# Encoder trunk on one core: the second half's root factors written as rows, and the pace of the last hidden pair

## Chip, cores and metric

One core of one Trainium2 chip. The metric is the time of one execution on the device in microseconds (us), as the median of several executions; three were made of the kernel before.

## What is computed

One layer of a streaming encoder for 2048 prompt frames and 32 sample frames of 1024 channels, everything in float32. The reference, cut to what matters here:

```python
def rmsnorm(x, g):
    y = x * lax.rsqrt(jnp.mean(x * x, axis=-1, keepdims=True) + EPS)
    return y * g

def layer(x, ...):
    h = rmsnorm(x, g_pre_mix)
    z = h @ w_in                      # u | zq | zf | zi | zg
    y_pool = pool_mix(u_ext, ...)     # trailing means over 2/4/8/16 frames, a 128x128 map per group
    S1, o = hgrn_run(S0, q, kin, zi, logf)   # gated recurrence in chunks, 4 heads of 128
    y_hg = rmsnorm(o, g_hg_norm) * silu(zg)
    x = x + rmsnorm(concat([y_pool, y_hg]) @ w_out, g_post_mix)
    h2 = rmsnorm(x, g_pre_ffn)
    f = (silu(h2 @ w_gate) * (h2 @ w_up)) @ w_down
    return x + rmsnorm(f, g_post_ffn)
```

The number that this case turns on is the root of the first `rmsnorm`: one factor `1/sqrt(mean(x*x) + EPS)` for each frame.

## The kernel before

The frames go through in two halves of 1024 frames (the second with the 32 sample frames beside it). For each half: the normed input in channel layout, split into a high and a low float32r part (`hT`); the value columns of `w_in` (`first_values` for the first half, `values` for the second); for each of 4 heads the gate, query and output-gate columns and the recurrence (`head_products`, `hgrn`); the pooling groups (`pool_products`); the projection by `w_out` in two groups of four tiles and two column halves (`project`, L1025); and gate and up of the feed-forward by a seven-product scheme (`gate_up`, L1201). When both halves are done, `down` (L1496) multiplies by `w_down`. A float32 product is made of three float32r matmuls of 128x512 each.

**Order of the work.** TensorE's instructions stand in the order in which the Python code emits them. `mm` (L199) and `tick` (L196) add a planned duration to a counter, `Pace.t`, and every third matmul calls `poll` (L224), which lets each side task (a generator in a `Task`, L206) go one step when the time that it yielded has passed on that counter. The other engines' instructions and the DMA issues of SP are not bound to that order: the tile framework's scheduler puts them in the order in which it expects them to be ready, with their place in the code as priority. So a `yield` fixes where a step's TensorE instructions stand, and only moves the rest. Buffers come from pools: four PSUM banks from `mmbank`, four from `axbank` (L101), 21 slots of 128x512 from `t2` (L107).

**The roots.** For the first half they are made on the fly. For the second half a side task, `later_stats` (L465), runs during the first half: it loads the frames, sums their squares on ScalarE, and computes on GpSimd a tile `st[:, 24:32]` of 128x8, in which element (p, i) is the root of frame 128 i + p. It is written to a DRAM row `roots` (L489), and the 32 roots of the sample frames behind it (L490). In `front_norm` (L516) of the second half the row is loaded back, broadcast to all partitions (`rb`, L521), and VectorE multiplies the channels by it (`scaled_channels`, L506). Before L489 the task waits 100 us of the counter for nothing but its turn.

**The hidden factors.** When a pair of blocks of gate and up is done, `hidden` (L1156) makes from its four tiles the seven left factors of the down product: sums on VectorE (L1164 to L1174), a high part on ScalarE (`hhi`, L1178), a low part on VectorE (`hlo`, L1181), and a store of each to DRAM by SP (L1183, tiles `hdFalse` and `hdTrue` for the two halves). `gate_up` takes one such step in each slot; what is left at its end, 19 steps in either half, goes to a side task, `flush` (L1414), one step every 1400 ns of the counter. For the first half that task runs beside `values` of the second half, for the second half beside the start of `down`, whose left factors SP loads as `hst` (L1506).

In `values` (L648) the four PSUM banks of the first 512 frames must be copied out (L670, `va` and `vb`, two by ScalarE and two by VectorE) before the same four banks take the next 512 frames.

Of the kernel before, what the change touches and what calls it, by code (L numbers as in the profile page):

```python
# [16 lines left out]
P = 128  # L17
# [6 lines left out]
HALF = 1024  # L24
# [13 lines left out]
NCH = HALF // CHUNK  # L38
# [40 lines left out]
def body(tc, ins, outs, cst):  # L79
    nc = tc.nc  # L80
    ctx = ExitStack()
    with ctx:
# [18 lines left out]
        def axbank(name="axb"):  # L101
            return AX.tile([P, 512], F32, tag="ax", name=name)
# [4 lines left out]
        def t2(name, shape=None, dt=F32):  # L107
            return TP.tile(shape or [P, 512], dt, tag="t", name=name)
# [4 lines left out]
        ident = cons[:, C_ID:C_ID + P]  # L113
# [39 lines left out]
        roots = DP.tile([1, TMAX], F32, name="roots")  # L153
# [42 lines left out]
        def tick(ns):  # L196
            Pace.t += ns
# [120 lines left out]
        def sumsq(src, r, st):  # L318
            junk = SP.tile([P, D], BF16, tag="junk", name="junk", bufs=1)
            nc.scalar.activation(junk[0:r, 0:src.shape[1]], src, AF.Square, accum_out=st)  # L320
# [144 lines left out]
        def later_stats(S):  # L465

            st = S.st
            for i in range(NCH):
                for c in range(2):
                    x = t2("xtl")  # L470
                    r0 = S.tok0 + i * P
                    nc.sync.dma_start(out=x, in_=x_p[r0:r0 + P, c * 512:c * 512 + 512])
                    sumsq(x, P, st[:, 2 * i + c:2 * i + c + 1])
                    del x
                yield 20000.0
            xs = t2("xsl", [NS, 512]), t2("xsl", [NS, 512])
            for c in range(2):
                nc.sync.dma_start(out=xs[c], in_=x_s[:, c * 512:c * 512 + 512])
                sumsq(xs[c], NS, st[0:NS, 32 + c:33 + c])
            del xs  # L480
            yield 100000.0
            ev = st[:, 0:16].rearrange("p (i c) -> p i c", c=2)
            nc.gpsimd.tensor_tensor(st[:, 16:24], ev[:, :, 0], ev[:, :, 1], ALU.add)
            nc.gpsimd.tensor_scalar(st[:, 16:24], st[:, 16:24], 1.0 / D, EPS, ALU.mult, ALU.add)
            nc.gpsimd.tensor_tensor(st[:, 24:32], st[:, 16:24], nhalf[:, 0:1].broadcast_to([P, NCH]), ALU.pow)
            nc.gpsimd.tensor_tensor(st[0:NS, 34:35], st[0:NS, 32:33], st[0:NS, 33:34], ALU.add)
            nc.gpsimd.tensor_scalar(st[0:NS, 34:35], st[0:NS, 34:35], 1.0 / D, EPS, ALU.mult, ALU.add)
            nc.gpsimd.tensor_tensor(st[0:NS, 35:36], st[0:NS, 34:35], nhalf[0:NS, 0:1], ALU.pow)
            nc.sync.dma_start(out=roots[0, 0:HALF].rearrange("(i p) -> p i", p=P), in_=st[:, 24:32])  # L489
            nc.sync.dma_start(out=roots[0, HALF:TMAX].rearrange("(p i) -> p i", i=1), in_=st[0:NS, 35:36])  # L490

        def scaled_channels(S, tg):
# [708 lines left out]
        def gate_up(S, on_last):  # L1201
# [175 lines left out]
            def job():  # L1377
                if jobs and next(jobs[0], 0) == 0:
                    jobs.pop(0)
# [34 lines left out]
            def flush():  # L1414
                while jobs:
                    job()
                    yield 1400.0

            Task(flush())

        def residual(row0, r):
# [266 lines left out]
        with tc.manual_schedule(engines={mybir.EngineType.PE}):  # L1688
            for i, S in enumerate(halves):
                if i:  # L1690
                    while S.seen[0] < 1:
                        S.norm[0].step()
                    values(S, 0)
                    values(S, 1)
                if i == 0:
                    halves[1].st = CP.tile([P, 64], F32, name="st_b")
                    Task(later_stats(halves[1]), 25000.0)
                    Task(mixed_weights(), 4000.0)
                for h in range(NH):
                    head_products(S, h)  # L1700
                for g in (3, 2, 1, 0):
                    pool_products(S, g)
                S.gpm = row_vector("g_post_mix")
                for tg in range(2):
                    project(S, tg)
                gate_up(S, second_start if i == 0 else (lambda: down_first(halves)))
            down(halves)
            for tk in list(Pace.tasks):
                tk.finish()
# [40 lines left out]
```

## Time and profile before

| what | us |
|---|---|
| median of 3 executions | 2109.58 |
| lowest, highest | 2109.41, 2110.47 |
| the profiled execution's own time | 2110.55 |
| its span, first to last instruction | 2108.8 |

| engine | busy us | share of the span |
|---|---|---|
| TensorE matmul (PE) | 2081.5 | 99% |
| TensorE weight load (PEld) | 1690.4 | 80% |
| VectorE (DVE) | 1423.5 | 68% |
| ScalarE (ACT) | 831.6 | 39% |
| GpSimd (POOL) | 283.4 | 13% |

The profile is of one execution. "Idle before" in brackets is the time that an engine stood still before an instruction, with what ended that wait; "issue" means that nothing which the profile records ended it. PEclk is the clock that TensorE was granted, as a share of full speed: 1.00 is 2.4 GHz and 0.50 is 1.2 GHz. The DMA share is the mean busy share of the core's 16 DMA engines. SP's own rows are the issues of DMAs and not the transfers.

### The profile page before, as it was taken

The page shows a single profiled execution, that of the slowest core. Times are in us where ns is not written, and L with a number is a line of the kernel's source. Part 1 is how long each engine was busy: PE and PEld are TensorE (multiplying, and loading weights), DVE is VectorE, ACT ScalarE, POOL GpSimd, SP SyncE. Part 2 cuts the span into 40 slices and gives each one's busy share as a digit, 9 for nine tenths or more (in the row PEclk, how much of TensorE's full clock was granted, in tenths as well). Part 3 has the DMA queues.
Part 4 walks back from the last instruction along what each step waited for, and adds up shares of the span by engine and source line. Part 5 has one row for each costly group of instructions (what it writes and reads, how often), then busy time and mean ns, then how long its engine had stood idle before and what let it go on. Part 6 is the DMA issues. An engine that isn't in the chain of part 4 may idle for free.

```text
span 2108.8 us, 34100 instructions
## 1 busy us (share of the span) xinstructions
PE 2081.5 (99%) x13117; PEld 1690.4 (80%) x13117; DVE 1423.5 (68%) x2302; ACT 831.6 (39%) x1659; POOL 283.4 (13%) x387
## 2 busy tenths in 40 slices
PE   9999899999999999999999999999999999999998
PEld 8788688888888887778878788888888778888876
DVE  6565575797777778456575687767666856566587
ACT  6444344654444445233333664444444521011032
POOL 1132302200000000022231210000000301110134
PEclk9999999999999999999999999999999999999999
DMA  9321142626555557310014524545455796776778
GB/s 322 111 72 51 34 150 96 194 86 176 162 155 155 150 175 229 112 45 25 23 36 162 188 93 130 156 141 148 147 148 151 241 311 207 225 225 196 223 224 215
DMA packets 394242, 321.07 MB, mean 152 GB/s; under 512 B 19144, under 2 KB 321472, under 8 KB 394080
## 3 DMA queue, kind: packets, MB, share of 16 engines
q1 hardware_dynamic: 391632, 310.98, 47.9%
q0 software_dynamic: 2016, 7.34, 1.9%
q8 instruction: 104, 1.70, 0.3%
q10 hardware_dynamic: 432, 0.57, 0.1%
q14 instruction: 58, 0.48, 0.1%
HBM read 218.36 MB, written 100.47 MB: 151 GB/s over the span
## 4 chain that ended last, share of the span: by engine, by line
PE 88%; DVE 6%; issue 2%; DMA 1%; ACT 1%; POOL 1%; SPq 0%; DVEq 0%; POOLq 0%; ACTq 0%
PE gx L200 21%; PE mmb L200 15%; PE gy L200 10%; PE dx L200 10%; PE ops L200 10%; PE gz L200 5%; PE dy L200 5%; PE vps L200 3%; PE dz L200 2%; PE gb L200 1%; DVE acc L1533 1%; PE gw L200 1%; PE gsps L200 1%; PE ups L200 1%; PE tps L343 1%
## 5 line engine op out<-in xcount | busy, mean ns | idle before, releaser
L200 PE MATMUL gx<-fhi,wf 128*128 128x512 f32 x1376 | 387.3, 391 | 0.0
L200 PEld LDWEIGHTS gx<-fhi,wf 128*128 128x128 f32 x1376 | 256.6, 188 | 55.3 <-issue 3.0
L200 PE MATMUL gx<-flo,wf 128*128 128x512 f32 x688 | 213.0, 390 | 0.0
L200 PE MATMUL gy<-fhi,wf 128*128 128x512 f32 x704 | 201.8, 390 | 0.1
L200 PE MATMUL dx<-dhi,hst 128*128 128x512 f32 x640 | 185.3, 391 | 0.8 <-DVE acc L1533 0.6
L200 PE MATMUL mmb<-hTlo,whi 128*128 128x512 f32 x512 | 177.4, 407 | 0.0
L200 PE MATMUL mmb<-hThi,whi 128*128 128x512 f32 x512 | 166.4, 406 | 5.6 <-issue 5.6
L1533 DVE TENSOR_TENSOR acc<-dx,acc 128x512 f32<-128x512 f32 x168 | 115.0, 689 | 72.9 <-PE dx L200 72.1
L1256 DVE TENSOR_TENSOR wf<-s,wf 128x512 fp32r<-128x512 f32 x176 | 119.9, 687 | 60.6 <-ACT wf L1251 58.3
L200 PE MATMUL mmb<-hThi,wlo 128*128 128x512 f32 x512 | 159.9, 394 | 0.0
L200 PEld LDWEIGHTS gy<-fhi,wf 128*128 128x128 f32 x704 | 131.7, 188 | 28.5 <-DVE c L1355 0.8
L200 PEld LDWEIGHTS gx<-flo,wf 128*128 128x128 f32 x688 | 129.1, 188 | 27.0
L1251 ACT CAST wf<-s 128x512 fp32r<-128x512 f32 x176 | 108.3, 621 | 102.5 <-DVE s L1232 31.5
L200 PEld LDWEIGHTS dx<-dhi,hst 128*128 128x128 f32 x640 | 119.5, 188 | 30.0 <-issue 3.4
L1256 DVE TENSOR_TENSOR wf<-wraw,wf 128x512 fp32r<-128x512 f32 x132 | 89.6, 686 | 40.2 <-ACT wf L1251 40.2
L200 PEld LDWEIGHTS mmb<-hThi,whi 128*128 128x128 f32 x512 | 91.6, 189 | 27.3 <-issue 10.0
L200 PEld LDWEIGHTS mmb<-hTlo,whi 128*128 128x128 f32 x512 | 96.6, 189 | 21.1 <-issue 1.3
L200 PEld LDWEIGHTS mmb<-hThi,wlo 128*128 128x128 f32 x512 | 96.9, 189 | 19.5 <-issue 0.7
L1472 ACT CAST dhi<-t 128x1024 fp32r<-128x1024 f32 x20 | 20.6, 1052 | 232.2 <-DVE dlo L1473 163.7
L1251 ACT CAST wf<-wraw 128x512 fp32r<-128x512 f32 x132 | 80.8, 621 | 73.9 <-PE gx L200 37.4
L200 PE MATMUL gy<-flo,wf 128*128 128x512 f32 x352 | 108.7, 389 | 0.0
L200 PE MATMUL dy<-dhi,hst 128*128 128x512 f32 x320 | 98.6, 389 | 1.1 <-DVE acc L1533 1.1
(327 smaller groups left out, 3998.0 us busy)
## 6 DMA issues: line engine op xcount, KB each, us to landing
hst<-hdFalse SPq DMA_DIRECT2D x140, 256.0 KB, 3.0
hst<-hdTrue SPq DMA_DIRECT2D x140, 256.0 KB, 3.0
wraw<-in_w_gate_dram SPq DMA_DIRECT2D x50, 512.0 KB, 4.2
wraw<-in_w_up_dram SPq DMA_DIRECT2D x50, 512.0 KB, 4.0
hdFalse<-hhi SPq DMA_DIRECT2D x77, 256.0 KB, 2.3
hdFalse<-hlo SPq DMA_DIRECT2D x77, 256.0 KB, 2.5
hdTrue<-hhi SPq DMA_DIRECT2D x77, 256.0 KB, 2.6
hdTrue<-hlo SPq DMA_DIRECT2D x77, 256.0 KB, 2.5
```

The costliest lines, as they stand in the source:

```text
L200: nc.tensor.matmul(out, l, r, start=start, stop=stop, skip_group_check=more)
L343: nc.tensor.transpose(ps[:, c:c + P], xn[:, (2 * kp + kk) * P:(2 * kp + kk + 1) * P], ident)
L1251: nc.scalar.copy(wf[:, 0], getattr(M, src) if isinstance(src, str) else src)
L1256: nc.vector.tensor_tensor(wf[:, 1], getattr(M, src) if isinstance(src, str) else src, wf[:, 0].bitcast(F32), ALU.subtract)
L1472: nc.scalar.copy(hi, src)
L1533: nc.vector.tensor_tensor(dst, ps, dst, ALU.add)
```

## The change

Two edits. The tile of roots is no longer written by one DMA that takes its 1024 floats one by one. TensorE transposes it into an `axbank`, ScalarE copies the 8x128 result to a `t2` tile, and a DMA writes it as 8 rows of 512 bytes; the transpose comes 3000 ns of the counter after the old place of the step. And `flush` takes a step every 2800 ns of the counter where it took one every 1400; the code is one function for both halves.

```diff
@@ later_stats @@
             nc.gpsimd.tensor_tensor(st[0:NS, 35:36], st[0:NS, 34:35], nhalf[0:NS, 0:1], ALU.pow)
-            nc.sync.dma_start(out=roots[0, 0:HALF].rearrange("(i p) -> p i", p=P), in_=st[:, 24:32])
+            yield 3000.0
+            ps = axbank("rps")
+            nc.tensor.transpose(ps[0:NCH, 0:P], st[:, 24:32], ident)
+            tick(107)
+            rows = t2("rows", [NCH, P])
+            nc.scalar.copy(rows, ps[0:NCH, 0:P])
+            nc.sync.dma_start(out=roots[0, 0:HALF].rearrange("(i p) -> i p", p=P), in_=rows)
             nc.sync.dma_start(out=roots[0, HALF:TMAX].rearrange("(p i) -> p i", i=1), in_=st[0:NS, 35:36])
@@ gate_up @@
             def flush():
                 while jobs:
                     job()
-                    yield 1400.0
+                    yield 2800.0
```

## Rows read from the trace of the kernel before

**Rows 1.** The page, part 1: busy time and share of each engine.

```profile
PE 2081.5 (99%) x13117; PEld 1690.4 (80%) x13117; DVE 1423.5 (68%) x2302; ACT 831.6 (39%) x1659; POOL 283.4 (13%) x387
```

**Rows 2.** Waits of PE over the span: us in total, times, longest.

```profile
PE mmb L200 <- issue: 5.6, 1, 5.6
PE gb L200 <- issue: 3.5, 2, 3.1
```

**Rows 3.** Timeline of PE, 236 to 251 us: start, length, instructions, idle before.

```profile
236.16 0.44 PE L200 MATMUL gb<-qa,k_t 128*32 128x16 f32 x31 [0.35 <-issue]
239.72 0.80 PE L200 MATMUL gb<-qa,k_t 128*32 128x16 f32 x33 [3.12 <-issue]
...
247.72 1.22 PE L200 MATMUL mmb<-hThi,whi 128*128 128x512 f32 x2 [5.63 <-issue]
...
250.58 0.75 PE L200 MATMUL gb<-qa,k_t 128*32 128x16 f32 x64
```

**Rows 4.** Windows of 2 us: busy PE, PEld, DVE, ACT, POOL; PEclk, DMA share, GB/s.

```profile
236.00:238.00 2.00, 0.44 (x31) 0.38 (x32) 0.61 (x2) 0.00 (x0) 0.00 (x0) 1.00 0.26 17
...
242.00:244.00 2.00, 0.09 (x1) 0.00 (x0) 1.42 (x2) 0.00 (x0) 0.27 (x1) 0.50 1.00 348
```

**Rows 5.** Timeline of SP's DMA issues, 215 to 275 us.

```profile
229.30 0.38 SPq L489 DMA_DIRECT2D roots<-st_b  x1
```

**Rows 6.** DMA in 229 to 242 us: packets; then issues, KB, us to landing.

```profile
DMA packets 1526, 0.25 MB, mean 19 GB/s; under 512 B 1040, under 2 KB 1526, under 8 KB 1526
...
wraw<-in_w_in_dram SPq DMA_DIRECT2D x1, 512.0 KB, 14.2
```

**Rows 7.** DMA in 242 to 250 us: the queue that brings instructions.

```profile
q8 instruction: 2, 0.03, 1.5%
```

**Rows 8.** DMA of the whole span: issues of the same load.

```profile
wraw<-in_w_in_dram SPq DMA_DIRECT2D x32, 512.0 KB, 5.3
```

**Rows 9.** Windows of 4 us, columns as in rows 4.

```profile
836.00:840.00 4.00, 2.75 (x7) 2.14 (x8) 4.00 (x6) 3.96 (x8) 0.00 (x0) 0.72 0.54 156
...
848.00:852.00 4.00, 4.00 (x22) 2.36 (x22) 0.43 (x1) 0.00 (x0) 0.00 (x0) 1.00 1.12 330
```

**Rows 10.** Timeline of PE, 833 to 842 us.

```profile
833.89 0.61 PE L200 MATMUL vps<-wlw,hThi 128*128 128x512 f32 x2
834.34 0.61 PE L200 MATMUL vps<-whw,hTlo 128*128 128x512 f32 x2
837.25 0.85 PE L200 MATMUL vps<-whw,hThi 128*128 128x512 f32 x2 [2.29 <-ACT va L670]
...
841.23 0.63 PE L200 MATMUL vps<-whw,hTlo 128*128 128x512 f32 x2
```

**Rows 11.** Timeline of ACT, 834 to 838 us.

```profile
834.77 1.28 ACT L507 CAST hThi<-xT 128x512 fp32r<-128x512 f32 x2 [1.84 <-DVE xT L506]
836.09 0.62 ACT L1178 CAST hhi<-hs 128x512 fp32r<-128x512 f32 x1
836.61 0.58 ACT L670 COPY va<-vps 128x512 f32<-128x512 f32 x1
```

**Rows 12.** Timeline of DVE, 820 to 836 us.

```profile
820.30 1.41 DVE L506 SCALAR_TENSOR_TENSOR xT<-xT,cons,rb 128x512 f32<-128x512 f32 x2 [5.61 <-DMA rb<-roots]
...
824.30 0.69 DVE L1181 TENSOR_TENSOR hlo<-hs,hhi 128x512 fp32r<-128x512 f32 x1
...
832.79 0.68 DVE L1181 TENSOR_TENSOR hlo<-c,hhi 128x512 fp32r<-128x512 f32 x1
```

**Rows 13.** Timeline of PE: eight transposes of 128x128 in a row.

```profile
263.76 1.03 PE L902 MATMUL kps<-cons,k_t 128*128 128x128 f32 x8
```

**Rows 14.** Timeline of ACT, 367 to 371 us.

```profile
370.70 0.60 ACT L320 ACTIVATE junk<-ops 128x512 bf16<-128x512 f32 x1 [2.17 <-DVE ym L1057]
```

**Rows 15.** Windows of 10 us at the start of `down`, columns as in rows 4.

```profile
1660.00:1670.00 10.00, 9.18 (x40) 6.96 (x39) 9.77 (x17) 6.41 (x12) 0.00 (x0) 1.00 0.60 181
...
1700.00:1710.00 10.00, 9.54 (x49) 6.88 (x41) 7.58 (x10) 5.40 (x8) 0.00 (x0) 1.00 0.98 303
```

## The prediction

> **What bounds the kernel.** I read the busy shares first: TensorE works through 99% of the span, every other engine through less than 70% [rows 1]. So work that the change moves to ScalarE, VectorE or SP is worth nothing by itself, and only two things can change the time: stretches in which TensorE stands still, and stretches in which its clock is down. TensorE's waits come next. Apart from the two ends of the span, two places stand out.
>
> The first is a wait for "issue", 5.6 us once and 3.5 us in two pieces [rows 2]. Nothing that the profile records ended it. The timeline puts all of it between 236 and 248 us, and the longer piece of the 3.5 us falls inside a run of 64 like matmuls, 31 before it and 33 behind [rows 3]: a semaphore has no business there, so what was missing must be the instructions themselves. The granted clock fell to 0.50, which is 1.2 GHz, after the first standstill [rows 4]. Now look at what else happens: SP issues the store of the roots at 229.30 [rows 5]. From 229 to 242 us the DMA engines move 0.25 MB, in 1040 packets of under 512 bytes among others [rows 6], which are about the 1024 single floats of that store. A weight load issued just behind it lands after 14.2 us [rows 6], where this load needs 5.3 us in the median of the whole run [rows 8]. The two packets of the instruction queue come only after 242 us [rows 7], while the queued loads rush in at 348 GB/s [rows 4]. I read this as one event: the store of single floats stops up the DMA engines, and TensorE's next block of code is stuck behind it.
>
> The second is at 834 us: 2.29 us idle until ScalarE has copied `va` [rows 10], and then the clock is at 0.72 in the mean of 4 us, partly at the lower level [rows 9]. The first bank of `values` could be copied while TensorE still fills the others. But ScalarE does things in its queue's order: ahead of `va` stand two `hThi` casts that wait for VectorE's `xT`, and one `hhi` of the hidden factors [rows 11]. VectorE in turn starts on this late, because the broadcast `rb` came late, and works without a pause from 820.30 on; between there and the last `xT` at 834 stand five operations of the hidden factors, of 0.68 us each; the rows show the first and the last of the five [rows 12].
>
> **A: the store as eight rows.** What goes is the whole of the first event. From the end of the idle 0.35 us at 236.16 to 250.58 us are 14.42 us, and in them stand 64 small matmuls and 9 large ones: the pair at 247.72 and seven between the rows [rows 3]. At full clock 64 such take 0.75 us, as at 250.58 [rows 3], and large ones come every 0.225 us, two between 833.89 and 834.34 [rows 10], so 9 take 2.03. Due: 2.78 us. **A = 2.78 - 14.42 = -11.6 us**, of which 8.75 are the two standstills and the rest the low clock. The 0.35 us may be an ordinary wait for VectorE, so I leave it in. All of it lies on TensorE, hence on the path. Eight rows of 512 bytes in place of 1024 floats put hardly anything before the next load. Lower end of the gain: nothing (rival 2). Upper end: 11.6 + 0.35 = 12.0.
>
> A rule of the Trainium skill speaks against this, in "Runtime: NRT & Kernel Launch", section "Instruction fetch mechanics": an engine's code comes in blocks by a DMA queue of the sequencer's own, the next block while the current one runs, and that cost is mostly hidden. By it A would be 0, since nothing could starve. The trace agrees for the rest of the span, where I find no other such wait, and disagrees at 236 us, where the standstill falls inside a run of like matmuls [rows 3].
>
> **C: the transpose and its copy.** One small matmul more: eight of 128x128 take 1.03 us [rows 13], so 0.13 us. It stands where the counter says, by the kernel's own charges added up less than 1 us before the last quarter of the first half's projection, about 368 us on the trace of before. That quarter takes all four `axbank` banks, so its fourth accumulator may wait for ScalarE to empty the new one; it is first written some 18 matmuls, 4 us, into the quarter. ScalarE has 2.17 us free right there [rows 14], and I take the copy of 128 columns as no longer than the 0.60 us of its neighbour with 512. Ends: 0.1 if it goes into that gap, 2.4 if it slips behind the four squares that follow (4 x 0.6). I take **C = +0.1**, since the gap is at hand. On SP the new store waits for this copy; behind it stand weight loads that are fetched several blocks ahead, so I cost that at nothing, and at the 2.4 us above if that cover is gone. The 32 sample roots are still written singly; they are a thirty-second of the floats.
>
> **B: the pace.** Nothing is removed: the 19 steps left of the pair are spread over twice the counter's time. Of the five hidden operations on VectorE between 820.30 and 834 us about half then come later, 2 or 3 x 0.68 = 1.4 to 2.0 us, and the `hhi` ahead of `va` (0.52, from 836.09 to 836.61 [rows 11]) with them. That takes 1.9 to 2.5 us from a wait of 2.29 [rows 10], and a wait well under 1 us has left the clock at 1.00 elsewhere, at 1700 us [rows 15]. What the low clock costs: from 837.25 to 841.23 us pass 3.98 us for 10 matmuls, two in each of five rows [rows 10], 2.25 at full clock, so 1.7 us. Ends: 0 (the scheduler puts VectorE's work in an order of its own and the wait stays) and 2.29 + 1.73 = 4.0. I take **B = -3.5**, nearer to the full gain, since the two amounts above almost close the wait. The steps that come later fall where VectorE is busy 0.43 of 4 us, at 848 [rows 9], so nothing is late next.
>
> **D: the same pace at the start of `down`.** The diff's function serves both halves. In 1660 to 1670 us VectorE is busy 9.77 of 10 us and TensorE loses 0.82, in 1700 to 1710 it loses 0.46 [rows 15]. Fewer hidden steps at once help the first, steps that last longer can hurt the second. **D = 0**; ends -1.3 (both gone) and +2 (as much again as was lost, and a half).
>
> **Sum.** The profiled execution took 2110.55 us. 2110.55 - 11.6 - 3.5 + 0.1 = 2095.55; it lies 0.97 us above the median of the runs, so 2094.6 for the median of the changed kernel. About 0.2%, 4.2 us, is what a measurement can tell from no change.
>
> **Rival 1: the pace gives nothing** (20%). B = 0: VectorE's order is the scheduler's and not the counter's, and the late `rb` is not touched. Then 2098.1, up to 2102 with the bad ends of C and D. For it: the hidden steps already run well behind their place. Against: ScalarE's order in [rows 11] shows `hhi` directly ahead of `va`.
>
> **Rival 2: the store isn't what held TensorE** (5%). The code block is late for another reason, such as the bulk loads that run at the same time, so A = 0 and only B and C are left: 2094.6 + 11.6 = 2106.2, within 0.2%. For it: the 5.63 us stretch lies over the bulk loads at 348 GB/s rather than over the single floats [rows 3, 4]. Against: at 848 us the DMA engines are as full, 330 GB/s, and TensorE loses nothing [rows 9]. It is what the page on the runtime, quoted above, would lead to.
>
> **Rival 3: slower, by SP's queue at the start of `down`** (3%). SP issues in order, and each store of a hidden factor waits there for its `hlo`. At half pace the stores reach 19 x 1.4 = 26.6 us further into `down`, among the `hst` loads that TensorE needs next. If each store held a load back until TensorE waits, the price is up to those 26.6 us, and the time 2094.6 + 26.6 = 2121. It decides only from 19 us on (15 gained, 4 that count), so almost every store would have to do so. Against: SP fetches several products ahead.
>
> That the change doesn't do what it says is part of rival 1: the pace is asked of the counter alone.
>
> **Numbers.** The forecast has 72%, with 2092 to 2097 as its own range. The range 2092 to 2101 takes in rival 1 and the ends of C and D; rivals 2 and 3 lie outside. Faster: 72 + 20 = 92%. Same: rival 2, 5%. Slower: rival 3, 3%.
>
> **What would show it.** A right: no wait for "issue" in TensorE's list, the clock at 1.00 throughout 230 to 260 us, and the load behind the old place of the store landing in about 5 us. A wrong: the same wait in the same place, or one at the new place of the store near 357 us. B right: the wait for `va` under 0.6 us and no dip of the clock behind it; wrong if 2 us stand there again. C wrong if TensorE waits for ScalarE in the projection near 360 us. D: losses between 1650 and 1710 us other than 1 to 2 us. Over 2102 us the sum has failed; under 2092 something gave that I do not see.

## The result and the profile after

The changed kernel takes **2097.24 us**, the median of four executions (2096.89 to 2097.60), against 2109.72 for the kernel before beside it (2109.41 to 2110.47): ratio 0.9939, with an interval of 0.9927 to 0.9951. It is faster by 12.5 us. The forecast was 2094.6 with a range of 2092 to 2101.

The profiled execution took 2097.60 us: 2094.6 of span and 3.00 outside it. Before these were 2108.8 and 1.75. First the page, part 1, which answers to [rows 1], then TensorE's longest waits, which answer to [rows 2] (us in total, times, longest):

```profile
PE 2077.1 (99%) x13118; PEld 1690.4 (81%) x13118; DVE 1424.7 (68%) x2302; ACT 832.2 (40%) x1660; POOL 282.6 (13%) x387
```

```profile
PE gb L200 <- DVE qa L808: 1.9, 5, 0.7
PE gy L200 <- DVE c L1361: 1.2, 2, 0.6
PE dy L200 <- DVE acc L1539: 1.1, 1, 1.1
...
PE tps L343 <- ACT ym L1096: 0.6, 1, 0.6
...
PE gb L200 <- issue: 0.4, 1, 0.4
```

The 5.6 and 3.5 us of waits for "issue" are gone, and no wait for `va` is listed. (Below L489 the lines stand six further down.) The windows say the same of the clock: 1.00 where it was 0.50 [rows 4] and, at the place of the second event, where it was 0.72 [rows 9]. Columns as there:

```profile
230.00:240.00 10.00, 9.46 (x274) 7.26 (x275) 8.28 (x16) 4.19 (x10) 4.05 (x3) 1.00 0.01 3
240.00:250.00 10.00, 10.00 (x117) 7.82 (x107) 5.86 (x17) 3.74 (x14) 6.71 (x15) 1.00 0.03 2
824.00:828.00 4.00, 4.00 (x19) 3.32 (x18) 4.00 (x7) 3.48 (x6) 0.00 (x0) 1.00 0.35 97
```

The timeline of TensorE shows the place of [rows 3]. Where it took from 236.16 to 250.58 us from one run of 64 small matmuls to a later one, it now takes from 236.63 to 239.55:

```profile
236.63 0.73 PE L200 MATMUL gb<-qa,k_t 128*32 128x16 f32 x64 [0.33 <-DVE qa L808]
...
239.55 0.74 PE L200 MATMUL gb<-qa,k_t 128*32 128x16 f32 x64
```

That is 2.92 us in place of 14.42, so 11.5 less. The DMA view of 225 to 245 us shows what else came back: four packets of the queue that brings instructions. The kernel before has no packet of that queue in the same stretch, only its own 2439 (second fence):

```profile
q1 hardware_dynamic: 290, 0.40, 6.6%
q8 instruction: 4, 0.07, 2.1%
```

```profile
q1 hardware_dynamic: 2439, 1.18, 28.0%
```

**Where the 14.2 us of span went.** The same instructions on both timelines, after against before: 0.5 us later at 230 us, 11.0 earlier behind the first event, 10.9 at the start of `gate_up`, 9.4 at 436 us behind two waits that were not there (`tps` 0.55 and `gy` 0.62), 13.7 behind the second event, 13.2 at 1638 us (`gy` again, 0.55), 14.2 at the end. Then 1.25 us are lost outside the span: 12.95 from execution to execution.

### The profile page after: what moved, and what is told of

Read it like the earlier page. It is cut to its first block, busy times and chain, and to the rows that moved or that the text cites. A ratio compares the mean times of both kernels' runs of the same rounds, so it can differ in the third digit from the quotient of the medians.

```text
span 2094.6 us, 34092 instructions
## 1 busy us (share of the span) xinstructions
PE 2077.1 (99%) x13118; PEld 1690.4 (81%) x13118; DVE 1424.7 (68%) x2302; ACT 832.2 (40%) x1660; POOL 282.6 (13%) x387
## 4 chain that ended last, share of the span: by engine, by line
PE 92%; DVE 4%; issue 1%; ACT 1%; DMA 1%; POOL 1%; DVEq 0%; POOLq 0%; SPq 0%; ACTq 0%
PE gx L200 22%; PE mmb L200 15%; PE gy L200 11%; PE dx L200 11%; PE ops L200 10%; PE dy L200 5%; PE gz L200 5%; PE vps L200 4%; PE dz L200 3%; PE gb L200 1%; PE gw L200 1%; PE gsps L200 1%; PE ups L200 1%; DVE acc L1539 1%; PE tps L343 1%
```

## The experiments

e1 to e8 ran on one chip, e9 to e12 on another of the same kind. The kernel before, run beside them, took 2108.91 us (13 runs) for e1 to e4, 2108.49 (7 runs) for e5 to e8 and 2107.59 (one run) for e9 to e12. One number for a kernel means one run. `spare` is one more DRAM row, made beside `roots`.

### The two halves of the change: e1, e2, e7 and e8

e1 is the changed kernel with the old pace, e2 the old kernel with the new pace, e7 the changed kernel with the new pace for the first half alone (`S.B` is the second half). e8 is the changed kernel itself once more.

```diff
 e1, from the kernel after
-                    yield 2800.0
+                    yield 1400.0
 e2, from the kernel before
-                    yield 1400.0
+                    yield 2800.0
 e7, from the kernel after
-                    yield 2800.0
+                    yield 1400.0 if S.B else 2800.0
```

> The roots as rows, the old pace of 1400. If the store of single floats held up TensorE's code, the wait for issue at 236 us and the clock dip behind it are gone and the 2.3 us wait for va at about 820 to 835 us stays, with its dip: the span is 11 to 12 us under that of before, the time 2098 to 2099.5. If the store is innocent, the wait for issue stays and the time is 2109 to 2110. If the code block that arrives after the last instruction of the changed kernel comes from the added instructions, the time lies about 3 us above the span here too (1.8 us before).

> The pace of 2800, the store of single floats as before. If pace and store act apart from each other, the wait for issue stays (5.6 and 3.5 us, clock at 0.50 behind) and only the wait for va and its dip go: span about 3.5 us under before, time 2106 to 2107. If the pace gives nothing, 2109.7. If the late code block at the end comes from the instructions that the transpose adds, the time lies 1.8 us above the span, as before.

> The changed kernel with the pace of 2800 in the first half alone; the second half's steps, beside the start of down, go at 1400 as before. If the pace costs something there, 0.5 to 1.5 us less than the changed kernel, and fewer waits of TensorE between 1630 and 1710 us; if it helps there, as much more; if it does nothing, the same within 0.5 us.

> The changed kernel itself once more, on the chip of these runs, to set the others against: 2096.5 to 2098, TensorE's wait for va under 0.6 us, time about 3 us above the span.

| kernel | us, median | ratio to before, interval |
|---|---|---|
| e1, rows alone | 2097.74 (4 runs) | 0.9945, 0.993 to 0.9959 |
| e2, pace alone | 2107.12 (10 runs) | 0.9992, 0.9982 to 1.0001 |
| e7, rows, pace in the first half | 2097.28 (4 runs) | 0.9946, 0.9931 to 0.9961 |
| e8, the change again | 2096.55 (4 runs) | 0.9942, 0.9925 to 0.9958 |

The rows alone bring 11.2 us (2108.91 - 2097.74). The pace brings 1.8 by e2 and 1.2 by e8 against e1, and the interval of e2 reaches 1. e2 keeps the first event whole:

```profile
PE mmb L200 <- issue: 5.1, 1, 5.1
PE gb L200 <- issue: 2.9, 3, 2.2
```

e1 came out 0.3 us below what was expected of it, since the wait for `va` did not stay (see e9); e2, expected some 3.5 us under the kernel before, brought half of that.

The median of e7 stands between e1 and e8, inside their scatter, 0.7 us above e8: the times do not tell whether the pace matters at the start of `down`. The profiles do, by little. First the kernel before, then e7, waits of TensorE from 1630 to 1725 us:

```profile
PE dx L200 <- DVE acc L1533: 0.5, 1, 0.5
```

```profile
PE dx L200 <- DVE acc L1539: 0.5, 1, 0.5
```

This wait of 0.5 us stands in the four profiles with the old pace in the second half (before, e9, e1, e7) and in none of the ten with the new one. On the same instructions, e8 gains 0.9 us on e7 between 1640 and 1695 us.

### The wait for `va` again: e9

e9 is the kernel before, profiled a second time, without an edit.

> The kernel before once more, with a profile, on the chip of the other runs: is its wait for va the same in another execution? If it is fixed by the order of the work, 2.3 us and a clock dip stand there again. If it hangs on when the broadcast rb happens to land (VectorE waited 5.6 us for it in the first profile, 3.6 to 4.6 in the others), it differs from execution to execution, and by as much as rb is earlier. Time 2107 to 2111.

It took 2107.5 us, with a span of 2105.4 against 2108.8 in the profile that the prediction read. The waits of TensorE:

```profile
PE mmb L200 <- issue: 5.5, 1, 5.5
PE gb L200 <- issue: 3.0, 2, 2.6
...
PE vps L200 <- ACT va L670: 0.4, 1, 0.4
```

The first event is the same as before. The wait for `va` is 0.38 us and not 2.29 [rows 10], and the clock has no dip behind it. What differs is when VectorE gets `rb`. Its first `xT` in e9, in e1 and in the kernel after (timelines of DVE), with the idle time before it in brackets; it was 5.61 in [rows 12]:

```profile
818.18 1.41 DVE L506 SCALAR_TENSOR_TENSOR xT<-xT,cons,rb 128x512 f32<-128x512 f32 x2 [4.34 <-DMA rb<-roots]
```

```profile
807.45 1.42 DVE L512 SCALAR_TENSOR_TENSOR xT<-xT,cons,rb 128x512 f32<-128x512 f32 x2 [3.95 <-DMA rb<-roots]
```

```profile
809.60 1.42 DVE L512 SCALAR_TENSOR_TENSOR xT<-xT,cons,rb 128x512 f32<-128x512 f32 x2 [4.62 <-DMA rb<-roots]
```

Now set ScalarE's timelines beside these: e1, with the old pace, and then the kernel after.

```profile
821.98 1.28 ACT L513 CAST hThi<-xT 128x512 fp32r<-128x512 f32 x2 [1.85 <-DVE xT L512]
823.30 0.62 ACT L1184 CAST hhi<-hs 128x512 fp32r<-128x512 f32 x1
823.83 0.58 ACT L676 COPY va<-vps 128x512 f32<-128x512 f32 x1
```

```profile
823.47 0.62 ACT L513 CAST hThi<-xT 128x512 fp32r<-128x512 f32 x1 [1.93 <-DVE xT L512]
824.00 0.58 ACT L676 COPY va<-vps 128x512 f32<-128x512 f32 x1
```

With the old pace two `hThi` casts and then `hhi` stand directly ahead of `va`, as in [rows 11]; with the new one only a single `hThi`. Count from the first `xT` to the copy of `va`:

| pace | kernel | from first `xT` to `va` | idle before first `xT` | wait of TensorE for `va` |
|---|---|---|---|---|
| old | before | 16.31 us | 5.61 | 2.29 |
| old | e9 | 16.32 | 4.34 | 0.38 |
| old | e1 | 16.38 | 3.95 | none listed |
| new | e2 | 14.64 | 3.64 | none listed |
| new | after | 14.40 | 4.62 | none listed |
| new | e8 | 14.40 | 5.33 | none listed |

So the pace does bring `va` forward, by 1.7 to 2.0 us, in every execution of the table. It is worth something at this place only in one in which `rb` lands so late that TensorE would have waited. At 5.33 us, close to the 5.61 of the profile before, the new pace leaves no wait.

### Is the store the cause? e4, e3, e5

e4 is the changed kernel with the old store of 1024 floats put back at its old place, into a spare row that nothing reads. The roots still go out as rows.

```diff
 e4, in later_stats
+            nc.sync.dma_start(out=spare[0, 0:HALF].rearrange("(i p) -> p i", p=P), in_=st[:, 24:32])
             yield 3000.0
```

> The changed kernel with one more store: the same 1024 single floats to a spare row at the place where the kernel before wrote them (229 us); nothing reads it. If the store held up the code, the standstill is back at 236 us with the clock dip: 11 to 12 us more than the changed kernel, time 2108 to 2109. If the store is innocent, 2097 to 2098 and no wait for issue.

It took 2108.02 us, and the first event is there again:

```profile
PE mmb L201 <- issue: 5.4, 1, 5.4
PE gb L201 <- issue: 2.6, 2, 2.2
```

So the old store is the cause, whatever else the change does: the floats themselves, or SP's wait for them and the burst of loads behind it, which e11 below tells apart.

e3 keeps the transposes out of the question: it turns the roots there and back and stores the 1024 single floats late, at 357.04 us, in the projection. e5 puts a spare store of 1024 single floats into the second half's second head, which has the same mixture of small and large matmuls as the place of the first event, at 931.08 us.

```diff
 e3, in later_stats
-            yield 3000.0
+            yield 1000.0
...
-            nc.sync.dma_start(out=roots[0, 0:HALF].rearrange("(i p) -> i p", p=P), in_=rows)
+            yield 1200.0
+            ps = axbank("rps")
+            nc.tensor.transpose(ps[:, 0:NCH], rows, ident[0:NCH, 0:NCH])
+            tick(107)
+            back = t2("back", [P, NCH])
+            nc.scalar.copy(back, ps[:, 0:NCH])
+            nc.sync.dma_start(out=roots[0, 0:HALF].rearrange("(i p) -> p i", p=P), in_=back)
 e5, in hgrn
             tc_ = merge(0, f_t)
+            if B and h == 1:
+                dm = small("dm", [P, NCH], bufs=1)
+                nc.gpsimd.tensor_copy(dm, qa[:, 0:NCH])
+                nc.sync.dma_start(out=spare[0, 0:HALF].rearrange("(i p) -> p i", p=P), in_=dm)
```

> The roots go through two transposes, to rows and back, and are written as 1024 single floats again, at about 357 us where the changed kernel writes its rows. If a store of single floats stops TensorE wherever it stands, 9 us of waiting and a clock dip stand at 357 us and the time is about 2109. If it stops TensorE only where a block of code runs out while the DMA engines are stopped up, then little or nothing is lost here, in the projection, where TensorE runs long matmuls and the trace of before shows one instruction packet in some 30 us against one in 4 to 5 us around 236: time 2097 to 2098. If the store is innocent, 2097 to 2098 too; the run beside it tells these apart.

> The changed kernel with 1024 single floats written to a spare row at another place: in the recurrence of the second half's second head, where the code runs through runs of 64 small matmuls as at 236 us. If what counts is that code runs out fast there, a wait for issue of 5 to 9 us stands in that head (between 880 and 960 us), the clock dips behind it, and the time is 2104 to 2109. If 236 us was a place of its own (its weight loads, its code block), no wait for issue and 2097 to 2099.

e3 took 2102.69 us, which is neither of the times that were expected. Its DMA view of 358 to 370 us and a piece of TensorE's timeline:

```profile
wraw<-in_w_gate_dram SPq DMA_DIRECT2D x2, 512.0 KB, 15.2
```

```profile
392.53 0.27 PE L343 MATMUL tps<-cons,ym 128*128 128x128 f32 x1
396.24 0.90 PE L343 MATMUL tps<-cons,ym 128*128 128x128 f32 x3 [3.44 <-ACT ym L1102]
```

In the kernel after the loads of `in_w_gate_dram` land after 6.3 us, in the same window. The DMA engines are stopped up here as well, but TensorE has no wait for "issue": in this stretch the kernel after has no packet of the instruction queue either, so none was due. The bill comes 36 us later and by another road. SP is held at a single weight load from 358.78 to 367.09, the loads of the frames (`xr`) behind it come late, and TensorE waits 3.44 us for `ym`, with its clock at 0.50 behind the wait.

e5 took 2102.53 us, less than the 2104 to 2109 that were expected, with a wait of 3.95 us where 5 to 9 were:

```profile
943.75 0.40 PE L201 MATMUL mmb<-hThi,wlo 128*128 128x512 f32 x1
948.10 0.79 PE L201 MATMUL mmb<-hThi,wlo 128*128 128x512 f32 x1 [3.95 <-issue]
```

No other kernel has a wait for "issue" here. The load behind the store takes 13.8 us, and from 932 to 945 us there is no packet of the instruction queue, where the kernel after has two. The event can be made at another place, then, by the same store, though smaller. A store of rows was not tried at this place.

### What is it about the store? e6, e10, e11, e12

Four more spare stores at the old place, all in the kernel after: 256 single floats, the same 1024 floats in 128 pieces of 32 bytes, eight full rows (made by GpSimd, so that SP waits for it as it did before and the same burst of loads is queued behind), and 32 single floats.

```diff
 e6
+            nc.sync.dma_start(out=spare[0, 0:256].rearrange("(i p) -> p i", p=P), in_=st[:, 24:26])
 e10
+            nc.sync.dma_start(out=spare[0, 0:HALF].rearrange("(p i) -> p i", i=NCH), in_=st[:, 24:32])
 e11 (`full`, 8x128, is made and set to zero at the start of the task)
+            nc.gpsimd.tensor_copy(full[:, 0:NCH], st[0:NCH, 24:32])
+            nc.sync.dma_start(out=spare[0, 0:HALF].rearrange("(i p) -> i p", p=P), in_=full)
 e12
+            nc.sync.dma_start(out=spare[0, 0:NS].rearrange("(p i) -> p i", i=1), in_=st[0:NS, 24:25])
```

> The changed kernel with 256 single floats in place of 1024 written to a spare row at the old place. If the DMA engines are stopped up in proportion to the number of floats (about 11 us for 1024), they are free again after about 3 us, before the next block of code is needed: no wait for issue over 1 us, time 2097 to 2098.5. If it is the mere presence of such a store, the wait is back and the time is 2105 to 2109.

> The changed kernel with a spare store at the old place, of the same 1024 floats, but in 128 pieces of 32 bytes (8 floats of a partition side by side) in place of 1024 of 4. If short pieces as such stop up the DMA engines, the wait for issue is back and the time is 2105 to 2109; if it takes single floats of many partitions in one line of DRAM, no wait for issue and 2096.5 to 2098.

> The changed kernel with a spare store of 8 full rows of 512 bytes at the old place: SP waits there for GpSimd's roots as it did before, and the loads behind it go out in one burst after it, but the store has no short piece. If SP's wait and the burst of loads held up the code, the wait for issue is back, 2105 to 2109. If it was the floats, no wait for issue, 2096.5 to 2098.

> The changed kernel with 32 single floats at the old place, as many as the sample roots that are still written so. If any number of single floats stops the DMA engines for some 10 us (256 did as 1024 do), the wait for issue is back, 2105 to 2109. If it takes many, no wait for issue over 1 us and 2096.5 to 2098.

| spare store | us (one run each) | waits for "issue" | `wraw` there lands after | instruction packets, 230 to 242 us |
|---|---|---|---|---|
| none (e8) | 2096.55, median of 4 | none listed | 4.1 | 2 |
| e4, 1024 floats | 2108.02 | 8.0 | 13.9 us | 0 |
| e6, 256 floats | 2106.59 | 8.3 | 13.0 | 0 |
| e12, 32 floats | 2102.15 | 3.5 | 7.9 | 1 |
| e10, 128 pieces of 32 bytes | 2096.91 | 0.2 | 4.2 | 2 |
| e11, 8 rows of 512 bytes | 2096.74 | none listed | 3.8 | 2 |

In e8, which has no store there for SP to wait at, the load is the same one, issued at 216.25 us. The rows behind the table, e6 (its waits, then DMA from 230 to 242 us), e10 and e11 (the same DMA view), and e12 (the same DMA view, then its wait):

```profile
PE mmb L201 <- issue: 5.8, 1, 5.8
PE gb L201 <- issue: 2.5, 4, 1.0
```

```profile
wraw<-in_w_in_dram SPq DMA_DIRECT2D x1, 512.0 KB, 13.0
```

```profile
q8 instruction: 2, 0.03, 1.2%
...
wraw<-in_w_in_dram SPq DMA_DIRECT2D x1, 512.0 KB, 4.2
```

```profile
q8 instruction: 2, 0.03, 1.1%
...
wraw<-in_w_in_dram SPq DMA_DIRECT2D x1, 512.0 KB, 3.8
```

```profile
q8 instruction: 1, 0.02, 0.6%
...
wraw<-in_w_in_dram SPq DMA_DIRECT2D x1, 512.0 KB, 7.9
...
spare<-st_b SPq DMA_DIRECT2D x1, 0.1 KB, 4.4
```

```profile
PE mmb L201 <- issue: 3.5, 1, 3.5
```

I had thought of a cost per float. e6 refutes that: a quarter of the floats does nearly as much harm as all of them (10.0 against 11.5 us over e8), and 32 floats, for which neither expected time came, still do about half (2102.15 - 2096.55 = 5.6 us, and 5.2 against e10 on the same chip). e11 acquits SP's wait and the burst of loads, with which rival 2 falls. e10 writes the same 1024 values in pieces of eight, and nothing is left of the event: it is the single floats. The table also shows that the standstill goes with the missing instruction packets, kernel by kernel.

## Why the prediction was right, and where it was off

**A, right in place, mechanism and size.** Forecast -11.6, measured -11.5 on the same stretch of the two timelines, -11.2 by e1. The store of single floats stops up the DMA engines and TensorE's code comes late; e4, e5 and e6 make the event again, e10 and e11 do not. (What ended the first of the two standstills stays open, see the end.) The rule of the Trainium skill, in "Runtime: NRT & Kernel Launch", section "Instruction fetch mechanics", that the fetch of code is mostly hidden, holds for the rest of the span and fails here, in e2, e4, e6 and e12 at the same place, and in e5 at another. "A thirty-second of the floats" was a poor reason for letting the 32 sample roots go as they are: e12 shows that 32 single floats can cost 5.6 us. They are harmless here because SP issues them at 243.04 and nothing behind them before 253.81 (timeline of SP, the kernel after):

```profile
243.04 0.31 SPq L496 DMA_DIRECT2D roots<-st_b  x1
253.81 0.38 SPq L258 DMA_DIRECT2D wrow<-mixed  x1
```

That this gap is the reason is argued and not tried; nor was writing these 32 by rows too.

**C, right.** The transpose came at 356.57 us (forecast: near 357), and its copy 0.5 us after it (timelines of PE and ACT). TensorE waits for neither, and the same instructions run 0.10 us later behind it.

```profile
356.57 0.28 PE L491 MATMUL rps<-cons,st_b 128*8 128x128 f32 x1
```

```profile
357.36 0.24 ACT L494 COPY rows<-rps 8x128 f32<-8x128 f32 x1
```

**D, right in its sum, not in its parts.** Between 1630 and 1710 us TensorE loses 1.5 us; before it lost 1.6 from 1640 to 1720. But it is not the same loss. The wait of 0.5 us for `acc` (the 0.46 of [rows 15]) is gone with the new pace, and with the small gaps around it the same instructions gain 0.9 us. A wait for `gy` just ahead of them, 0.55 us where it was 0.05, takes half of that back; it lies between 0 and 0.99 us in the other profiles, also among those with the new pace, and what sets it is open. Of rival 3 there is no sign.

**B, right in its direction, wrong in size, and partly in its working: this is the term that was off.** The prediction took 1.9 to 2.5 us from the wait: two or three of VectorE's five hidden operations and the `hhi` ahead of `va`. `va` did come 1.7 to 2.0 us sooner, but by another sum. VectorE's last pair of `xT`, before and after (timelines of DVE):

```profile
833.99 1.41 DVE L506 SCALAR_TENSOR_TENSOR xT<-xT,cons,rb 128x512 f32<-128x512 f32 x2
```

```profile
822.69 1.41 DVE L512 SCALAR_TENSOR_TENSOR xT<-xT,cons,rb 128x512 f32<-128x512 f32 x2
```

From the first `xT` to this pair it was 13.69 us and is 13.09: four of the five hidden operations still stand between, so 0.60 us where 1.4 to 2.0 were forecast. The other 1.31 us (2.62 from this pair to `va`, now 1.31) were won on ScalarE, where not only `hhi` but also one of the two `hThi` casts no longer stands ahead of `va`. That the two sums agree is in part luck.

The larger error is the price. The prediction priced the gain at "a wait of 2.29" and the low clock behind it, as if they stood in each execution. They stood in the one that was profiled: e9, the same kernel, waits 0.38 us there and keeps its clock. From that profile to the one after, B gave 4.2 us (9.4 to 13.7 earlier), more than its 3.5. Over the runs the pace as a whole, with the start of `down`, brings 1.2 to 1.8 us, not told apart from nothing. So in the median rival 1 (2098.1) is not excluded.

**The 2.64 us between 2094.6 and 2097.24.** The forecast amounts to a span of 2108.8 - 15.0 - 0.97 = 2092.83 and 1.75 us outside it. The two middle executions had spans of 2094.5, so 1.65 of the miss lie inside the span and 0.99 outside. Inside, 0.8 is what the sum of -15.0 missed against the 14.2 of the two profiles: the new waits at 394 and 436 us took 1.5 us that stand in no term, and B gave 0.7 more than its own. The rest is the 0.97 that was taken off "for the median": the profiled execution lay above the median with the long wait for `va` in it, and the sum had already removed that wait. The same microseconds were, in part, taken off twice; that they are the same is argued from e9, not shown for each run. Outside, 1.75 was held constant, and it is not (below). In time the result lies nearer to rival 1 than to the forecast, and just past the forecast's own range of 2092 to 2097: it is the range of 2092 to 2101, which took in rival 1, that holds it.

## What to carry to other kernels

Write scattered values to DRAM in pieces, not as single floats: here 32 bytes a piece were enough, and a transpose of 0.3 us with a copy of 0.24 us saved 11 us. A DMA is not paid for by its bytes or by who waits for it alone: look which engine has code due, and which loads are queued, in the ten microseconds behind it. Before you price the removal of a wait, see whether it stands in a second profile; and when you then pass from one execution to the median, don't remove it again.

## What the runs showed of the hardware that was not expected

- 256 single floats stop the DMA engines up about as long as 1024 do (a load behind them lands after 13.0 and 13.9 us, without them after 3.8 to 4.2), and 32 floats for some 4 us; 128 pieces of 32 bytes do not. The Trainium skill says in "DMA: Bandwidth & Descriptors", section "Specifications", that below 512 bytes the engines read, modify and write; pieces of 32 bytes are below that too, so this alone does not separate them. Whether it is the size of a float, or that floats from many partitions fall next to each other in DRAM, is open.
- The first standstill ends at 239.72 us in the kernel before [rows 3], while no packet of the instruction queue is recorded there until after 242 us [rows 7]. What ended it is open.
- The time outside the span was 1.74 to 3.00 us in the fourteen profiled executions, with either kernel at both ends: 1.75 and 2.1 for the one before, 3.00 and 2.67 for the one after, and 1.74 in e11 and 2.92 in e4, which both are the one after with a spare store. e1 and e2 gave 2.2 and 1.78. What sets it was not settled.
